# A channel shuffle that streams 64 MB through SBUF: other tile sizes at its two ends

## The chip, the core and the metric

One of the eight cores of a Trainium2 chip runs the whole kernel. The metric is the device time of one execution in microseconds (us). Five executions of the kernel before gave a median of 317.01 us, with 316.95 us as the lowest and 317.26 us as the highest.

## The reference

The input `x` is a float32 array of 16 x 64 x 64 positions with 256 channels each, 67.11 MB in all. The 256 channels are 8 groups of 32. The result holds the same values with the two channel axes exchanged, at every position by itself:

```python
x = x.reshape(batch, h, w, groups, channels_per_group)   # 8 x 32
x = x.transpose(0, 1, 2, 4, 3)                           # 32 x 8
x = x.reshape(batch, h, w, c)
```

No arithmetic is done. Every byte has to be read from HBM once, be moved within its row of 256 channels, and be written to HBM once.

## The kernel before

The 65,536 positions are seen as rows of 256 floats, 1 KB each. The kernel cuts them into tiles of 128 x q rows: each of the 128 SBUF partitions gets q whole rows that lie next to each other in HBM, so a tile has q KB in each partition and 128 q KB in all. The list `_SIZES` on line 12 gives q for each tile in order, and its sum has to be 512 (65,536 / 128). There are 24 tiles before the change: 4, 8 and 16 KB a partition, then twenty of 24 KB (3.15 MB each), then one of 4 KB.

For each tile the loop does three things, in program order:

- line 47: SyncE's queue (SP) issues one transfer from HBM into `in_tile`;
- line 49: VectorE (DVE) copies `in_tile` to `out_tile` and exchanges the two channel axes by the order in which the copy reads;
- line 53: ScalarE's queue (ACT) issues one transfer from `out_tile` to HBM.

No other instruction works on the data. There are four `in_tile` buffers and four `out_tile` buffers, each as large as the biggest tile whatever the tile's size. So the first four loads are issued at once, and load k+4 waits until copy k has read its buffer. Copy k waits for load k to land, and, from the fifth tile on, for store k-4 to have left its buffer. Store k waits for copy k. Each queue issues in order: SP has only loads, ACT has only stores. The order of the program is the order in which the loop writes it; no scheduler moves anything.

The text numbers tiles, loads, copies and stores from 0 to 23. Each transfer is 128 packets, one for each partition's q KB, which are spread over the core's 16 DMA engines, 8 packets to each engine, and one packet of 4 bytes on each engine that reports the end. So the size of a tile is also the size of its packets.

Of the kernel before, what the change touches and what calls it, by code (L numbers as in the profile page):

```python
# [1 line left out]

# [4 lines left out]


F32 = mybir.dt.float32
P = 128  # L10

_SIZES = [4, 8, 16] + [24] * 20 + [4]
_IN_BUFS = 4
_OUT_BUFS = 4


@with_exitstack
def kernel(
    ctx: ExitStack,
    tc: tile.TileContext,  # L20
    x: bass.AP,
    groups: bass.AP,
    out: bass.AP,
):
    nc = tc.nc
    b, h, w, c = x.shape
    G = int(groups)
    CPG = c // G
    assert G * CPG == c
    assert sum(_SIZES) * P == b * h * w  # L30
    biggest = max(_SIZES)

    x_flat = x.rearrange("b h w c -> (b h w c)")
    out_flat = out.rearrange("b h w c -> (b h w c)")

    in_pool = ctx.enter_context(tc.tile_pool(name="in_pool", bufs=_IN_BUFS))
    out_pool = ctx.enter_context(tc.tile_pool(name="out_pool", bufs=_OUT_BUFS))

    def rows(flat, first, q):

        return flat[first * c : (first + P * q) * c].rearrange("(p f) -> p f", p=P)

    ctx.enter_context(tc.manual_schedule(engines=None))
    first = 0
    for q in _SIZES:
        in_tile = in_pool.tile([P, biggest * c], F32, name="in_tile")
        nc.sync.dma_start(out=in_tile[:, : q * c], in_=rows(x_flat, first, q))  # L47
        out_tile = out_pool.tile([P, biggest * c], F32, name="out_tile")
        nc.vector.tensor_copy(  # L49
            out=out_tile[:, : q * c].rearrange("p (i j g) -> p i j g", j=CPG, g=G),  # L50
            in_=in_tile[:, : q * c].rearrange("p (i g j) -> p i j g", g=G, j=CPG),
        )
        nc.scalar.dma_start(out=rows(out_flat, first, q), in_=out_tile[:, : q * c])
        first += P * q


# [1 line left out]
_INS = ['x', 'groups']  # L58
_OUTS = [((16, 64, 64, 256), 'float32')]

_NUMBERS = {'groups': 8}


# [26 lines left out]
```

## Time and profile before

| what | value |
|---|---|
| median of five runs | 317.01 us (316.95 to 317.26) |
| time of the profiled execution | 317.26 us |
| its span in the profile | 315.5 us |
| what lies around the span | 1.76 us |
| VectorE busy | 121.8 us (39%), 24 copies |
| bytes read and written | 67.11 MB each |
| mean rate over the span | 425 GB/s |
| DMA queues | q1 (loads, issued by SP) and q10 (stores, issued by ACT), 3456 packets each |

The profile counts time from the start of the span. Busy time of an engine is the time in which its instructions run; a DMA's issue on SP or ACT takes some 0.3 to 0.4 us and is not counted as busy, while its data moves for much longer, so a transfer is read by its issue and by its landing (the moment at which all 16 engines have reported its end). The rate in GB/s adds both directions.

### The profile page before, as it was taken

What the parts mean: (1) busy time and instruction counts of PE and PEld (TensorE: products, weight loads), DVE (VectorE), ACT (ScalarE), POOL (GpSimd) and SP (SyncE); (2) the same over time, 40 slices, a digit from 0 to 9 for tenths busy, and PEclk for the clock granted to TensorE, in tenths of its full rate; (3) what the DMA queues carried; (4) which work ended last, traced back from release to release, by engine and by line L of the source; (5) the groups of instructions that cost most, each with busy time, mean ns of one, the idle gap of its engine ahead of it and who ended that gap; (6) DMA issues with size and microseconds to landing.
All of it is one profiled execution on the core that took longest, in us unless ns stands there. A gap on an engine that the chain in (4) does not pass through costs nothing.

```text
span 315.5 us, 178 instructions
## 1 busy us (share of the span) xinstructions
DVE 121.8 (39%) x24; POOL 0.2 (0%) x4
## 2 busy tenths in 40 slices
DVE  3435716244251707061533526070715244261710
POOL 0000000000000000000000000000000000000000
DMA  8999999999999999999999999999999999999997
GB/s 316 415 404 428 440 424 446 433 418 446 433 418 446 436 414 446 436 414 446 436 421 439 442 414 439 446 418 433 449 414 433 449 421 427 449 424 427 441 420 319
DMA packets 6912, 134.22 MB, mean 425 GB/s; under 512 B 768, under 2 KB 768, under 8 KB 1280
## 3 DMA queue, kind: packets, MB, share of 16 engines
q1 hardware_dynamic: 3456, 67.11, 49.8%
q10 hardware_dynamic: 3456, 67.11, 49.5%
HBM read 67.11 MB, written 67.11 MB: 425 GB/s over the span
## 4 chain that ended last, share of the span: by engine, by line
DMA 36%; another core or an unknown queue 33%; DVE 26%; SPq 0%; issue 0%; DVEq 0%
DMA in_tile<-in_x_dram 36%; DVE out_tile L49 26%; SPq L47 0%; DVEq L49 0%
## 5 line engine op out<-in xcount | busy, mean ns | idle before, releaser
L49 DVE COPY out_tile<-in_tile 128x6144 f32<-128x6144 f32 (+3 forms) x24 | 121.8, 5075 | 181.6 <-DMA in_tile<-in_x_dram 181.6
L71 POOL MEMSET const-bfloat16-1.0<- 128x1 bf16 x1 | 0.1, 102 | 0.0
L71 POOL MEMSET const-uint8-127<- 128x1 uint8 x1 | 0.1, 102 | 0.0
L71 POOL MEMSET const-float32-0.0<- 128x1 f32 x1 | 0.1, 100 | 0.2 <-issue 0.2
L71 POOL MEMSET const-float32-1.0<- 128x1 f32 x1 | 0.1, 99 | 0.0
## 6 DMA issues: line engine op xcount, KB each, us to landing
in_tile<-in_x_dram SPq DMA_DIRECT2D x20, 3072.0 KB, 52.3
out_dram<-out_tile ACTq DMA_DIRECT2D x20, 3072.0 KB, 31.8
in_tile<-in_x_dram SPq DMA_DIRECT2D x1, 2048.0 KB, 11.0
out_dram<-out_tile ACTq DMA_DIRECT2D x1, 2048.0 KB, 23.8
in_tile<-in_x_dram SPq DMA_DIRECT2D x2, 512.0 KB, 24.8
in_tile<-in_x_dram SPq DMA_DIRECT2D x1, 1024.0 KB, 5.3
out_dram<-out_tile ACTq DMA_DIRECT2D x2, 512.0 KB, 11.9
out_dram<-out_tile ACTq DMA_DIRECT2D x1, 1024.0 KB, 19.1
```

The source lines that it names most:

```text
L49: nc.vector.tensor_copy(out=out_tile[:, : q * c].rearrange("p (i j g) -> p i j g", j=CPG, g=G), in_=in_tile[:, : q * c].rearrange("p (i g ...
L71: nc = _bacc.Bacc("TRN2", target_bir_lowering=False, num_devices=1)
```

## The change

The list of tile sizes is replaced. There are again 24 tiles that sum to 512. At the start the three tiles of 4, 8 and 16 KB become four of 2, 4, 8 and 18 KB; the twenty tiles of 24 KB follow; the last tile of 4 KB is gone, so the last tile is now one of 24 KB. The buffers, the loop, the engines and the queues are untouched.

```diff
-_SIZES = [4, 8, 16] + [24] * 20 + [4]
+_SIZES = [2, 4, 8, 18] + [24] * 20
 _IN_BUFS = 4
 _OUT_BUFS = 4
```

On VectorE the first four copies become 128 x 512, 128 x 1024, 128 x 2048 and 128 x 4608 elements where they were 128 x 1024, 128 x 2048, 128 x 4096 and 128 x 6144, and the last one becomes 128 x 6144 where it was 128 x 1024. The loads on SP and the stores on ACT change in the same way.

## The prediction

> **What bounds the kernel now.** I read the page first: the span, the rate in 40 slices, the bytes and the costliest group.
>
> ```profile
> span 315.5 us, 178 instructions
> GB/s 316 415 404 428 440 424 446 433 418 446 433 418 446 436 414 446 436 414 446 436 421 439 442 414 439 446 418 433 449 414 433 449 421 427 449 424 427 441 420 319
> HBM read 67.11 MB, written 67.11 MB: 425 GB/s over the span
> L49 DVE COPY out_tile<-in_tile 128x6144 f32<-128x6144 f32 (+3 forms) x24 | 121.8, 5075 | 181.6 <-DMA in_tile<-in_x_dram 181.6
> ```
>
> The rate is flat from the second slice to the last but one, and VectorE, the only engine with work, sits idle for 181.6 us until loads land. At 433 GB/s, the rate of the middle, 134.22 MB take 310 us of the span of 315.5. So the DMA engines are the bound, and what is left is 5.5 us at the two ends and in the ramp. To see where, I cut the span by stages:
>
> ```profile
> 1.60:6.00 4.40, 1.09 (x1) 0.00 (x0) 1.00 0.97 380
> 6.00:10.50 4.50, 2.02 (x1) 0.00 (x0) 1.00 1.04 400
> 10.50:18.00 7.50, 3.89 (x1) 0.00 (x0) 1.00 1.00 428
> 18.00:20.00 2.00, 0.00 (x0) 0.00 (x0) 1.00 0.97 377
> 20.00:40.00 20.00, 11.35 (x2) 0.00 (x0) 1.00 1.01 427
> 40.00:280.00 240.00, 91.84 (x17) 0.00 (x0) 1.00 1.00 433
> 302.00:312.00 10.00, 1.09 (x1) 0.00 (x0) 1.00 1.00 433
> ```
>
> The last number is GB/s. From 40 us on nothing is lost, whether loads and stores mix (40 to 280) or stores are alone (302 to 312). Before that the ramp falls short of 433. In time that is 4.50 x (1 - 400/433) = 0.34 us, 7.50 x (1 - 428/433) = 0.09, 2.00 x (1 - 377/433) = 0.26 and 20 x (1 - 427/433) = 0.28: together 0.97 us between 6 and 40 us. From 1.60 to 6 us it is 0.54 us, the first packets' latency among it.
>
> Then the end, since that is where the last tile grows. The timeline from 280 us:
>
> ```profile
> 284.87 18.85 ACTq L53 DMA_DIRECT2D out_dram<-out_tile  x3
> 293.70 5.69 DVE L49 COPY out_tile<-in_tile 128x6144 f32<-128x6144 f32 x1 [8.86 <-DMA in_tile<-in_x_dram]
> 302.27 1.09 DVE L49 COPY out_tile<-in_tile 128x1024 f32<-128x1024 f32 x1 [2.88 <-DMA in_tile<-in_x_dram]
> ```
>
> and the stores issued at 284.9, 299.4 and 303.4 us (tiles 21, 22, 23), each with its time to landing:
>
> ```profile
> L53 ACTq DMA_DIRECT2D out_dram<-out_tile x1: 339/339/339, 284.9 to 284.9; - x1
> DMA to landing us min/median/max: 21.3/21.3/21.3
> ...
> L53 ACTq DMA_DIRECT2D out_dram<-out_tile x1: 338/338/338, 299.4 to 299.4; - x1
> DMA to landing us min/median/max: 14.0/14.0/14.0
> ...
> L53 ACTq DMA_DIRECT2D out_dram<-out_tile x1: 338/338/338, 303.4 to 303.4; - x1
> DMA to landing us min/median/max: 11.3/11.3/11.3
> ```
>
> They land at 306.2, 313.4 and 314.7 us. Store 23 carries 0.52 MB, 1.2 us at 433 GB/s, and takes 11.3: it stands in a queue. How long that queue is, the bytes of each queue in the first 293.70 us (the landing of load 22) tell:
>
> ```profile
> q1 hardware_dynamic: 3313, 66.59, 53.1%
> q10 hardware_dynamic: 2959, 59.09, 46.8%
> ```
>
> The stores are 66.59 - 59.09 = 7.50 MB behind the loads. I call this the backlog.
>
> **The change part by part.** My sum is made against the profiled execution, 317.26 us: span 315.5 plus 1.76 around it. It stands 0.25 us above the median of 317.01, so a difference found there is applied to 317.0.
>
> *Bytes and packets: 0.* There are 24 tiles and 512 KB a partition before and after, so 48 transfers, 134.22 MB and 6912 packets. Only the split changes. The packet records of the trace have medians of 159, 309, 611 and 912 ns for packets of 4, 8, 16 and 24 KB: a straight line, 8.5 ns plus 37.6 ns a KB. On it 2 KB cost 84 ns and 18 KB 686. Each engine has 8 packets of each tile and direction: before (4 + 8 + 16 + 4 KB) 159 + 309 + 611 + 159 = 1238 ns, after (2 + 4 + 8 + 18) 84 + 159 + 309 + 686 = 1238. If the 2 KB packets kept the 4 KB price, 16 of them would add 16 x 75 ns = 1.2 us; if the line holds or bends down, 0. I take the line, as it holds over the three steps shown, the nearest at 4 KB; 1.2 us is the upper bound.
>
> *VectorE: 0.* The copies take 1.09, 2.02, 3.89 and 5.69 us for 4, 8, 16 and 24 KB, a straight line again, so about 0.6 for 2 KB and 4.3 for 18 KB. The sum of the changed copies goes from 8.1 us to 8.0. Each lies beside DMA work, as the 181.6 us of idle time show, save the last one, which has its own term.
>
> *The start: 0, at most +0.4 us.* Loads 0 to 3 are issued at 0.73, 1.14, 1.62 and about 2.1 us, 0.4 to 0.5 apart, and the first packet moves at 1.75, so an issue takes 1.0 us to show. Load 0 of 2 KB is 8 packets x 84 ns = 0.7 us plus the 0.3 us of first latency that the packet records show, to about 2.7; load 1 can move at 2.2. No hole. A hole could not be longer than one issue step, 0.4 us. The first four loads now hold 32 KB a partition where they held 52. Alone they feed the engines to about 1.75 + 0.3 + 8 x 1.238 = 12 us. Load 4 waits for copy 0, which is done by 4 us (it ended at 5.07 before, with a load twice as long), so load 4 is queued 7 us early. SP and ACT have no other work that could be held.
>
> *The ramp: +0.1 us, between -1.0 and +1.0.* The 0.97 us shown above sit where loads are alone (6 to 10.5 us) or outweigh stores (18 to 40 us). After the change both stages differ. Store 0 is issued at about 4.0 us in place of 5.1, so loads are alone for about 1 us less: at 400 GB/s a gain of 1 x 33/433 = 0.1 us. But the stores that then pair with loads are of 2, 4, 8 and 18 KB, one tile more before the two sides are equal, which lengthens the loads' majority: in the stage of 20 to 40 us that costs 0.28/20 = 0.014 us a us, and one more tile pair of 14.5 us makes +0.2. The bounds are that the whole loss goes (-1.0) or comes a second time (+1.0). I take the sum of the two small terms, since they come from the nearest rows.
>
> *The end: 0.* Here a 4 KB tile, copied in 1.09 us, is replaced by one copied in 5.69. The copy is on the path only if the store queue runs dry before the store is issued. The trace of before shows this very case one tile earlier. Load 22, of 24 KB, lands at 293.70, its copy takes 5.69 us, and store 22 is issued at 299.4. It lands 14.0 us later, while 3.15 MB need 7.3 at 433 GB/s. So some 6 us of the 14.0 are time in the queue; the packet records have its first packet at 305.04, 5.6 us after the issue. Without load 23 beside it (0.52 MB, 1.2 us) that spare would be 4.4 us.
>
> After the change the spare is larger, because the backlog grows. An engine that has both queues full takes a packet of each in turn. The end shows it: between 293.70 and 302.2 us load 23 of 0.52 MB takes 8.5 us, as 3.17 MB of stores pass beside it, packet for packet. So while a store tile of small packets pairs with loads of large ones, the backlog grows by 128 x the difference in KB. Before: 2.87 MB are loaded in the first 9 us without a store; store 0 (4 KB) meets loads of 16 and 24 KB, about +2.0 MB; store 1 (8 KB) meets 24, +2.1; store 2 (16) meets 24, +1.05. Sum 8.0 MB, and 7.50 were read above just after a load ended, with 24 KB on both sides it swings by half a tile. After: 2.4 to 2.9 MB alone; 2 KB against 18, +2.1; 4 against 24, +2.6; 8 against 24, +2.1; 18 against 24, +0.8. Sum 10.0 to 10.5 MB, or 3.2 to 3.3 tiles. When load 23 lands, at least 10.0 - 3.15 = 6.9 MB of older stores are left, 15.8 us at 433 GB/s, less 1.35 us in which load 22's last packet (292.35) became a landing. Copy 23 and its issue take 5.75 us, so store 23 stands in the queue 8.7 us before its turn. Even an issue that takes 4.1 us to show, as store 0's does (issued 5.1, first packet 9.18), leaves 4 us. Four out buffers hold 3.3 tiles, so copies don't wait for them either. The term runs from 0 to the cost of a dry queue in the rivals.
>
> The Trainium skill has a rule that speaks against this step: DMA: Bandwidth & Descriptors, section "Anatomy of one DMA — SWDGE (gpsimd) path", fits one transfer as about 2.0 us plus its bytes at 436 GB/s. As an estimate from that page the last store would go from 3.2 us to 9.2 and the kernel to about 323 us. The rows (11.3 us for 0.52 MB, 14.0 for 3.15) disagree with it: they are queueing times, and the fit is of the other issue path.
>
> The sum: 0 + 0 + 0 + 0.1 + 0 on 317.0, so **317.1 us**.
>
> **The rivals.**
>
> *The last copy is exposed.* If the two queues were not served packet for packet, or the stores caught up during the run, store 23 would find an empty queue. With nothing ahead of it the price is 1.35 + 5.69 + the 1.0 us that an issue takes, about 8 us less the 1.2 of the old small tile: 323.8 us. It decides from the point where the older stores left at load 23's landing fall under (5.75 + 1.0) x 0.433 = 2.9 MB. Before there were, at 293.70, 67.11 - 59.09 - 3.15 - 0.52 = 4.35 MB. A near miss would cost 1 to 2 us, 318 to 319. Against it stand the 5.6 us of spare.
>
> *The ramp gets worse.* More stages of lopsided traffic, or 2 KB packets at the old price, bring the 0.97 us a second time: 318.0 us. The loss from 18 to 20 us, beside a store of 8 KB packets, speaks for it; the 428 GB/s of 10.5 to 18 us, where a 4 KB store meets loads, speaks against it.
>
> *The ramp gets better.* The stage at 400 GB/s is that of the 16 KB load, which is gone. If its size were the cause, 0.34 us return; if the whole ramp loss goes, the time is 316.0 us. Against it: 24 KB loads lose time too, from 18 us on.
>
> **How the numbers follow.** Measured against the spread of these runs (0.1%), 0.2% or 0.63 us is about what can be told from no change: 316.4 to 317.6. No change 0.62; the ramp worse 0.17; the last copy exposed 0.08; the ramp better 0.13. So faster 0.13, same 0.62, slower 0.25. The range takes both bounds of the ramp and leaves out the exposed copy and what lies beyond the bounds: 316.0 to 318.2.
>
> **What would show it.** In the changed profile the last copy should start at about 292 to 293 us and the last store be issued near 298 and land some 16 us later, at the end. Stores of 24 KB should take about 41 us to land in the middle (31.8 before), loads 52.4 as before, and the middle run at 433 GB/s with 14.55 us from copy to copy. Stores should be about 10 MB behind loads. A rate under 420 GB/s in a stage between the last copy's start and the end would mean the exposed copy; one between 6 and 40 us that differs from the rows above, one of the ramp rivals. The prediction falls if the store queue empties before the last store, if 2 KB or 18 KB packets leave the line, or if a backlog of 10 MB changes the rate in the middle, where each 1% would be 3 us.

## The result, and the profile after

The changed kernel takes 317.74 us (median of 26 runs, 316.88 to 318.44) against 316.99 us before (46 runs, 316.77 to 317.39). The medians differ by 0.75 us. The ratio of the runs is 1.0022, with a 95% interval of 1.0017 to 1.0028 (0.5 to 0.9 us), at the edge of the 0.2% (0.63 us) that the prediction called "no change"; the median lies just outside it. The second finding is the spread: single runs of the changed kernel lie within 1.56 us, those of the kernel before within 0.62.

The profiled execution is one of the faster ones, 317.40 us; the one before, 317.26, is one of the slower ones of its kernel. So the two pages show little of the 0.75 us:

```profile
span 315.6 us, 178 instructions
HBM read 67.11 MB, written 67.11 MB: 425 GB/s over the span
L49 DVE COPY out_tile<-in_tile 128x6144 f32<-128x6144 f32 (+4 forms) x24 | 121.6, 5066 | 177.2 <-DMA in_tile<-in_x_dram 177.2
```

The stages of the changed kernel, cut as before (the last number is GB/s):

```profile
1.60:6.00 4.40, 1.51 (x2) 0.00 (x0) 1.00 0.99 359
6.00:10.50 4.50, 2.23 (x2) 0.00 (x0) 1.00 1.01 410
10.50:18.00 7.50, 3.97 (x1) 0.00 (x0) 1.00 1.01 430
18.00:20.00 2.00, 0.35 (x1) 0.00 (x0) 1.00 1.06 442
20.00:40.00 20.00, 11.35 (x2) 0.00 (x0) 1.00 1.01 420
40.00:280.00 240.00, 92.23 (x17) 0.00 (x0) 1.00 1.00 432
302.00:312.00 10.00, 0.00 (x0) 0.00 (x0) 1.00 1.01 435
```

The middle and the stores alone at the end run at the old rate (432 and 435 GB/s, 433 and 433 before). What differs lies before 40 us: 359 for 380 GB/s in the first stage, 410 for 400 in the second, 442 for 377 from 18 to 20 us, and 420 for 427 from 20 to 40 us.

The end, first in the timeline and then in the last store:

```profile
278.54 5.76 DVE L49 COPY out_tile<-in_tile 128x6144 f32<-128x6144 f32 x1 [8.85 <-DMA in_tile<-in_x_dram]
284.33 14.83 ACTq L53 DMA_DIRECT2D out_dram<-out_tile  x2
293.13 5.65 DVE L49 COPY out_tile<-in_tile 128x6144 f32<-128x6144 f32 x1 [8.84 <-DMA in_tile<-in_x_dram]
```
```profile
L53 ACTq DMA_DIRECT2D out_dram<-out_tile x1: 339/339/339, 298.8 to 298.8; - x1
...
DMA to landing us min/median/max: 16.0/16.0/16.0
```

The last load lands at 293.13, the copy takes 5.65 us, and store 23 waits in a queue: it lands 16.0 us after its issue, of which its 3.15 MB need 7.3. The bytes of the two queues in the first 293.13 us show the backlog:

```profile
q1 hardware_dynamic: 3456, 67.11, 53.7%
q10 hardware_dynamic: 3052, 58.36, 46.3%
```

The stores are 8.75 MB behind, 5.6 MB of it older than store 23. That is 12.9 us of work, and the copy needs 5.65. The packet records have store 23's first packet at 306.3 us, 7.5 us after its issue. So the last copy is not exposed.

**Where the time of an execution is made.** The packet records give each packet's duration, and packets of one size have one undisturbed duration, their median (912 ns for 24 KB). Packets that take longer are late. Added up over an execution and divided by 16 engines, in us an engine:

| execution | loads late, before 45 us | loads late, after 45 us | stores late, before / after 45 us |
|---|---|---|---|
| before, 317.26 | 1.19 | 0.0 | 0.0 / 0.0 |
| changed, 317.40 | 1.48 | 0.0 | 0.0 / 0.0 |
| changed again, 316.86 | 1.29 | 0.0 | 0.0 / 0.0 |
| changed a third time, 317.41 | 1.38 | 0.0 | 0.0 / 0.0 |

Only loads are late, and only at the start. From 45 us on 24 KB packets start 908 or 909 ns apart, and some 914 ns from one tile to the next, so what an engine has lost by then it keeps to the end. The sum of late time is not by itself the time lost: "changed again" has 0.10 us more of it than before, and yet its engines end earlier (next table), since its first packets begin 0.09 us earlier on average and the spaces between packets differ too. A store has landed when the last of the 16 engines reports it, so the engine that lost most sets the end:

| execution | mean of the 16 engines' last landings | last of the 16 | device time | device time less last landing |
|---|---|---|---|---|
| before | 314.11 | 314.67 | 317.26 | 2.59 |
| changed | 314.24 | 314.81 | 317.40 | 2.59 |
| changed again | 314.04 | 314.27 | 316.86 | 2.59 |
| changed a third time | 314.33 | 314.82 | 317.41 | 2.59 |

The 0.14 us between the two profiled executions and the 0.54 between two of the changed kernel are, to 0.01, the difference of the last engine's landing. The changed kernel can be as fast as the old one (316.86) when its 16 engines end together, within 0.45 us here.

### The profile page after: what moved, and what is told of

Its sections match the earlier page's. It is cut to its first block, busy times and chain, and to the rows that moved or that the text cites. A ratio compares the mean times of both kernels' runs of the same rounds, so it can differ in the third digit from the quotient of the medians.

```text
span 315.6 us, 178 instructions
## 1 busy us (share of the span) xinstructions
DVE 121.6 (39%) x24; POOL 0.2 (0%) x4
## 4 chain that ended last, share of the span: by engine, by line
another core or an unknown queue 42%; DVE 31%; DMA 21%; issue 0%; DVEq 0%
DVE out_tile L49 31%; DMA in_tile<-in_x_dram 21%; DVEq L49 0%
## 5 line engine op out<-in xcount | busy, mean ns | idle before, releaser
L49 DVE COPY out_tile<-in_tile 128x6144 f32<-128x6144 f32 (+4 forms) x24 | 121.6, 5066 | 177.2 <-DMA in_tile<-in_x_dram 177.2
## 6 DMA issues: line engine op xcount, KB each, us to landing
out_dram<-out_tile ACTq DMA_DIRECT2D x20, 3072.0 KB, 38.5
```

The lines of the kernel that those rows point to most:

```text
L49: nc.vector.tensor_copy(out=out_tile[:, : q * c].rearrange("p (i j g) -> p i j g", j=CPG, g=G), in_=in_tile[:, : q * c].rearrange("p (i g ...
```

## The experiments

The theories were: the small tiles at the start cost it ("head"), the 24 KB tile at the end costs it ("end"), or the twenty 24 KB tiles cost it because they now begin four blocks of 128 rows later ("rows"). Each batch shared the runs of the kernel before, with medians of 316.93 to 317.00 us.

### The new head with the old end

```diff
-_SIZES = [4, 8, 16] + [24] * 20 + [4]
+_SIZES = [2, 4, 8, 14] + [24] * 20 + [4]
```

> Sizes 2, 4, 8, 14, twenty of 24, then 4 KB: the new small head with the old 4 KB end, and the 24 KB tiles at the old rows. Theory 'head' (loads outweigh stores for longer at the start, and this costs the 0.7 us and the wider spread of the runs): about 317.6 us, spread of the runs over 1 us. Theory 'end' (a 24 KB last tile costs it): 317.0 us with a spread of 0.6 us. Theory 'rows' (the 24 KB tiles start 4 row blocks later): 317.0 us.

Measured: 317.93 us (9 runs, 316.90 to 318.07), ratio 1.0023 (1.0014 to 1.0033). The head alone brings the whole difference and the spread. In its profile (317.68 us) the stage from 20 to 40 us is again the one that is short, and the middle is not:

```profile
20.00:40.00 20.00, 11.42 (x2) 0.00 (x0) 1.00 1.01 420
40.00:280.00 240.00, 94.93 (x17) 0.00 (x0) 1.00 1.01 433
```

The last landings have a mean of 314.32 us, 0.21 later than before, but the last one is at 315.05, 0.38 later, with the next to last at 314.48. One engine alone makes over half a microsecond of this execution's time.

### The small tile moved from the end to the start

```diff
-_SIZES = [4, 8, 16] + [24] * 20 + [4]
+_SIZES = [4, 8, 16, 4] + [24] * 20
```

> Sizes 4, 8, 16, 4, then twenty of 24 KB: the old head, with the small last tile moved to the fourth place, so that the last tile is of 24 KB and the 24 KB tiles start at the changed kernel's rows. Theory 'head': near 317.0 us, unless the 4 KB tile beside 24 KB loads makes a lopsided stage of its own (then up to 317.6). Theory 'end': 317.7 us. Theory 'rows': 317.7 us.

Measured: 317.26 us (11 runs, 317.10 to 317.38), ratio 1.0009 (1.0000 to 1.0018). Neither 317.0 nor 317.7: by itself it could have meant a small cost of the end. Its packet records put its loss elsewhere: its 16 KB loads are late by about 0.55 us an engine between 9.5 and 12.5 us (before 0.06), and no 24 KB packet is late by more than 0.02 us.

### The changed kernel again, and the rows

The changed kernel was run again, and the old sizes were run on the new rows:

```diff
-    for q in _SIZES:
+    for k, q in enumerate(_SIZES):
+        if k == 3:
+            first = 32 * P
+        if k == 23:
+            first = 28 * P
```

> The changed kernel once more, for a second profile and a second set of times on the same chip as the others of this batch. All theories: 317.7 us with single runs between 316.9 and 318.5. If the time of the profiled execution is over 317.9, its packet records should show where it differs from the first profile (317.40): in the ramp by 'head', after the last load by 'end', in the middle by 'rows'.

> The sizes and the order of the kernel before, but the last tile of 4 KB takes the rows after the 16 KB tile, so the twenty 24 KB tiles start 4 row blocks later, at the rows where the changed kernel has them. Theory 'rows': 317.7 us. Theories 'head' and 'end': 317.0 us with the old narrow spread.

Measured: the changed kernel 317.61 us (11 runs, 316.86 to 318.67), ratio 1.0017 (1.0006 to 1.0027); the old sizes on the new rows 317.00 (316.78 to 317.08), ratio 1.0000 (0.9992 to 1.0009). "Rows" falls. The profiled execution was the fastest of them, 316.86, so it shows nothing of the longer ones.

### The end alone

```diff
-_SIZES = [4, 8, 16] + [24] * 20 + [4]
+_SIZES = [4, 8, 16] + [24] * 20
...
-    assert sum(_SIZES) * P == b * h * w
+    assert sum(_SIZES) * P <= b * h * w
```

> Sizes 4, 8, 16, then twenty of 24 KB, and nothing more: the last 4 KB a partition of the kernel before are left out (neither read nor written), so the old head meets a 24 KB end. The 16 packets of 4 KB that each engine no longer moves are 16 x 155 ns = 2.5 us. If a 24 KB end is free: 317.0 - 2.5 = 314.5 us, with the narrow spread of the kernel before. If the end costs the 0.3 us by which the kernel with the small tile in fourth place was slower: 314.8 us. If the end costs all of the 0.7 us: 315.2 us.

Measured: 314.62 us (5 runs, 314.52 to 314.63) against 316.96. Less 2.5 us for the work left out, 0.1 to 0.2 us remain for a 24 KB end. Most of that lies behind the last landing: device time less last landing is 2.73 us here and 2.72 in the two other kernels with 23 tiles (4, 8, 20 and 8, 12, 16, 20, below), where the kernels with 24 tiles have 2.58 to 2.60, three of them with a 24 KB end. Why 23 tiles cost 0.13 us there was not asked. Its own end, in the timeline and the last store, looks like the old kernel's tile 22:

```profile
293.80 5.70 DVE L49 COPY out_tile<-in_tile 128x6144 f32<-128x6144 f32 x1 [8.87 <-DMA in_tile<-in_x_dram]
299.53 0.34 ACTq L53 DMA_DIRECT2D out_dram<-out_tile  x1
```
```profile
DMA to landing us min/median/max: 12.4/12.4/12.4
```

Even with the smaller backlog of the old head the last store stands in a queue: 12.4 us to its landing for 7.3 us of data.

### Three small tiles, and a gentle head

```diff
-_SIZES = [4, 8, 16] + [24] * 20 + [4]
+_SIZES = [4, 8, 20] + [24] * 20
```
```diff
-_SIZES = [4, 8, 16] + [24] * 20 + [4]
+_SIZES = [8, 12, 16, 20] + [24] * 19
```

> Sizes 4, 8, 20, then twenty of 24 KB: 23 tiles, a 24 KB end, and a head in which 24 KB loads meet a store of 8 KB packets for one tile only, as before. Theory 'lopsided' (time is lost while 24 KB loads meet stores of 8 KB and less): 317.0 us less 0.1 for one tile's packets fewer, narrow spread. Theory 'end': 317.3 or more.

> Sizes 8, 12, 16, 20, then nineteen of 24 KB: 23 tiles and no stage in which 24 KB loads meet stores under 12 KB. Theory 'lopsided': 316.6 to 316.9 us, with almost no loss between 18 and 40 us. Its rival, that the loss is made where loads are alone and of 12 KB or more (load 0 is larger, so the first store comes about 2 us later): 317.2 us or more.

Measured: 4, 8, 20 gives 317.02 us (11 runs, 316.86 to 317.13), ratio 1.0002 (0.9993 to 1.0011), with a 24 KB tile at its end. With the run before this settles the end: it costs 0.2 us at most. The gentle head gives 317.28 (316.91 to 317.46), ratio 1.0009 (1.0000 to 1.0018). "Lopsided" expected 316.9 at most. Not one of its 24 KB packets is late, as that theory said, but its 16 and 20 KB loads are, by 0.65 us an engine from 9.5 to 14.5 us and 0.23 from 19.5 to 23.5. Its rival's time (317.2 or more) came, but not quite its place: only half of the late 16 KB load time, 0.33 us, falls before the first store's packets at 11.5 us, where loads are alone.

### Lopsided traffic far from the start

```diff
-_SIZES = [4, 8, 16] + [24] * 20 + [4]
+_SIZES = [4, 8, 16] + [24] * 7 + [2] + [24] * 6 + [2] + [24] * 7
```

> The kernel before with its last tile of 4 KB cut into two tiles of 2 KB and put far apart in the middle (after 7 and after 13 of the 24 KB tiles), so that two stages of some 8 us have 24 KB loads beside 2 KB stores, far from the start; two more packets a tile and engine add 0.1 us. Theory 'lopsided': each stage loses 0.1 to 0.4 us, so 317.3 to 317.9 us with a wide spread. Theory 'ramp alone' (the loss needs the state of the engines after the start, not the mix): 317.1 us, and no loss in the packet records of the two stages.

Measured: 317.07 us (11 runs, 316.99 to 317.32), ratio 1.0004 (0.9995 to 1.0012). The two small stores go out from 134 to 142 and from 223 to 231 us, beside 24 KB loads. The stages around them:

```profile
130.00:142.00 12.00, 6.50 (x2) 0.00 (x0) 1.00 1.02 438
142.00:219.00 77.00, 28.70 (x7) 0.00 (x0) 1.00 1.00 432
219.00:231.00 12.00, 6.48 (x2) 0.00 (x0) 1.00 0.98 421
231.00:290.00 59.00, 24.38 (x5) 0.00 (x0) 1.00 1.00 432
```

In such short windows the rate depends on which packets begin inside (the kernel before has 432 and 428 in the same two), so the packet records decide: between 45 and 300 us no packet is late by as much as 20 ns. Loads of 24 KB beside stores of 2 KB are not late by themselves. "Lopsided" by itself falls; the loss belongs to the start.

### What in the head: the 2 KB, or the fourth small tile

```diff
-_SIZES = [4, 8, 16] + [24] * 20 + [4]
+_SIZES = [4, 4, 8, 16] + [24] * 20
```
```diff
-_SIZES = [4, 8, 16] + [24] * 20 + [4]
+_SIZES = [2, 8, 18] + [24] * 20 + [4]
```

> Sizes 4, 4, 8, 16, then twenty of 24 KB: four small tiles as in the changed kernel, but the first is of 4 KB. The first 24 KB load is then the fifth, issued after copy 0, as in the changed kernel. Theory 'fourth small tile' (the loads run on through 24 KB packets while a fourth small store goes out, and the load packets that are late then cost the slowest engine): 317.5 to 317.8 us with a spread over 0.8 us. Theory 'first tile of 2 KB': 317.0 us, narrow.

> Sizes 2, 8, 18, twenty of 24, then 4 KB: three small tiles and the old end, but the first tile is of 2 KB. The first 24 KB load is the fourth, issued at once, as before. Theory 'first tile of 2 KB' (the first store comes a microsecond earlier and its small packets leave the engines out of step): 317.5 to 317.8 us, wide. Theory 'fourth small tile': 317.0 us, narrow.

Measured: 4, 4, 8, 16 gives 317.48 us (11 runs, 317.23 to 318.28), ratio 1.0019 (1.0010 to 1.0027), slower and wide without a 2 KB tile. Its profiled execution is one of the longer ones, 318.01 us, and shows the slowest engine at work: mean of the last landings 314.38, the last at 315.42, four others between 314.7 and 314.9. The other, 2, 8, 18, gives 317.14 (12 runs, 316.82 to 317.50 and one of 319.21), ratio 1.0010 (0.9999 to 1.0021): unclear, but nearer to the old kernel.

The third profile of the changed kernel, of a single execution:

> The changed kernel, one more profile, in the hope of an execution near its median of 317.7 us. What every theory left expects: no loss after 45 us, and the time above the fastest execution explained by the slowest of the 16 DMA engines: its last landing lies 2.6 us before the device time, as in the profiles so far (314.83 for 317.40, 314.29 for 316.86).

Its execution took 317.41 us, with the last landing at 314.82. The difference of 2.59 held (the expectation's two landings stand 0.02 us late against the profile's zero: they are 314.81 and 314.27); an execution of the changed kernel at or above its median was never profiled.

### A fifth small tile

```diff
-_SIZES = [4, 8, 16] + [24] * 20 + [4]
+_SIZES = [2, 2, 4, 8, 16] + [24] * 20
```

> Sizes 2, 2, 4, 8, 16, then twenty of 24 KB: five small tiles ahead of the 24 KB ones, where the changed kernel has four and the kernel before three; one tile more than the changed kernel adds 0.1 us of packets. Theory 'number of small tiles ahead' (each small tile adds a stage at the start in which the 16 engines lose unequal time, and the slowest sets the end): 318.0 us or more, spread over 1 us. Rival, that the step from three to four alone does it, since four loads are issued at once and the first 24 KB load is then no longer among them: 317.5 to 317.8 us, like the changed kernel. If five small tiles give 317.1, neither stands.

Measured: 318.35 us (5 runs, 317.74 to 318.64), ratio 1.0037 (1.0023 to 1.0050). Its first three stages and the long ones:

```profile
1.60:6.00 4.40, 1.23 (x2) 0.00 (x0) 1.00 0.93 244
6.00:10.50 4.50, 1.19 (x2) 0.00 (x0) 1.00 1.01 411
10.50:18.00 7.50, 3.91 (x2) 0.00 (x0) 1.00 1.03 436
...
20.00:40.00 20.00, 11.49 (x2) 0.00 (x0) 1.00 1.01 432
40.00:280.00 240.00, 96.29 (x17) 0.00 (x0) 1.00 1.01 433
```

and those of 4, 4, 8, 16:

```profile
1.60:6.00 4.40, 1.86 (x2) 0.00 (x0) 1.00 0.96 330
6.00:10.50 4.50, 1.81 (x2) 0.00 (x0) 1.00 1.03 380
10.50:18.00 7.50, 3.28 (x2) 0.00 (x0) 1.00 0.99 418
```

Here the loss is in the first 10 us (244 GB/s against 380 before), where the third and fourth of the small loads (4 and 8 KB) have late packets, up to 1.5 us late; 20 to 40 us is clean at 432. The mean of the last landings is 314.82, 0.71 later than before, and the last is at 315.71, 1.05 later. That is nearly the difference of the two profiled executions (318.35 and 317.26, 1.09). Late packets are only 0.36 us an engine of the 0.71; the packets of one more tile add 0.16, and the rest lies in the spaces between packets.

Set side by side, by the number of tiles under 24 KB ahead of the long run:

| small tiles ahead | heads, median us |
|---|---|
| 3 | 4, 8, 16: 316.99 (on other rows 317.00); 4, 8, 20: 317.02; 2, 8, 18: 317.14 |
| 4 | 4, 8, 16, 4: 317.26; 8, 12, 16, 20: 317.28; 4, 4, 8, 16: 317.48; 2, 4, 8, 18: 317.74; 2, 4, 8, 14: 317.93 |
| 5 | 2, 2, 4, 8, 16: 318.35 |

By their medians all heads of four are above all of three, and five is above all of four. The number is not all: within the four, those that begin with 2 KB are the slowest. And the two fastest heads of four, at 0.3 us more, have intervals that begin at 1.0000 and overlap with that of 2, 8, 18; only the other three, and the head of five, are clearly slower than the kernel before.

## Why the prediction was right or wrong

The time of 317.74 us lies in the range of 316.0 to 318.2. It is not in the likeliest case (316.4 to 317.6, chance 0.62) but between it and the rival "the ramp gets worse" (318.0, chance 0.17). That rival was near in time, but neither of its two reasons held: 2 KB packets kept to the line, and lopsided traffic in the middle lost nothing.

*Bytes and packets, 0:* right. The packet records of the changed kernel have medians of 84 ns for 2 KB and 686 for 18 KB, the values read off the line.

*VectorE, 0:* right. Copies of 0.63 and 4.32 us (0.6 and 4.3 foreseen), and the idle time is still all for loads.

*The end, 0:* right, and shown by the end alone (0.1 to 0.2 us) and by 4, 8, 20 with a 24 KB end (317.02). The last copy began at 293.13 (292 to 293 foreseen), its store was issued at 298.8 (298) and landed 16.0 us later (16). The backlog came out a little under the sum: in the packet records it is 9.4 to 10.1 MB in the middle (10.0 to 10.5 foreseen), 2.2 MB of it loaded ahead of the first store (2.4 to 2.9 foreseen), and 24 KB stores took 38.5 us to land where about 41 were foreseen. At the landing of load 23 it is down to 8.75 MB, since hardly anything but stores moves in the last 1.35 us before. The prediction's aside that the backlog swings by half a tile was too large: before, it ran from 7.5 to 8.3 MB, a quarter of a tile. The fit of a DMA's time in the Trainium skill (DMA: Bandwidth & Descriptors, "Anatomy of one DMA — SWDGE (gpsimd) path"), which by the prediction's estimate would have made it about 323 us, does not apply here: a last transfer six times as large added 0.2 us at most.

*The start, 0 to +0.4, and the ramp, +0.1 between -1.0 and +1.0:* this is the step that failed, in size. The ramp and the start together cost the 0.75 us, less the 0.2 at most of the end, where 0.1 was the sum. That lies within the bounds, which is owed to their width: the value taken was the sum of two small terms from the mean rate of the stages. The first, a gain of 0.1 for a shorter time with loads alone, and the second, +0.2 for one more lopsided tile pair, have the right sign and are too small: in late load time the changed kernel's three profiles (executions of 316.9 to 317.4 us, under its median) have 0.13 to 0.22 us an engine from 6 to 10.5 us (before 0.48) and 0.55 to 0.74 from 20 to 40 us (0.23). A third, in the first stage up to 6 us, was put at nothing and is 0.35 to 0.56 (0.27). The reason given, lopsided traffic, is not enough: it loses nothing far from the start. The loss goes with late load packets of the first 45 us, at places that differ from head to head (9.5 to 12.5 us for 4, 8, 16, 4; before 10 us for 2, 2, 4, 8, 16), and the end is set by the engine that lost most, not by the mean. A mean rate can't show that: in the execution of the new head with the old end, 0.21 us of the 0.38 us are seen in the mean, the rest in one engine.

*The spread:* not foreseen. The prediction took the profiled execution, 0.25 us above its median, as good for the whole. For the changed kernel one profile is worth less: its three lay 0.3 to 0.9 us below its median of 317.74.

*What stays open:* why load packets are late at the start and never later. The place was found, a fourth small tile was clearly slower in three heads of five, and the mix of sizes far from the start was shown to cost nothing. Whether it is the reading of HBM, the preparing of so many transfers in so short a time, or the order in which the engines fall out of step was not told apart. Nor was the number of small tiles separated from the fact that the first 24 KB load is then no longer among the four issued at once; the fifth small tile speaks for the number, as it cost more again, but it starts with two tiles of 2 KB. All five heads of four have that late first 24 KB load and range from 317.26 to 317.93, so it does not set the size of the loss alone. That the slowest engine makes the changed kernel's own longer executions, and so the 0.75 us of its median, is argued from neighbours (317.68, 318.01 and 318.35 us), since its own profiles were all of faster executions.

## What to carry to other kernels

In a stream that the DMA engines bound from end to end, the last copy and store cost nothing while older stores still queue ahead of them, so read the queue at the last load's landing before shrinking the last tile. At the start, do not add small tiles beyond what fills the pipe: here no head of three was clearly slower than the kernel before, three of five heads of four were, and the one of five was the slowest. Fewer than three were not tried. And where 16 engines share a transfer, look at the last of them and at several executions: the mean rate of one profile hides both.

## What was not expected of the hardware

After the first 45 us the DMA engines were exact to a few nanoseconds: 24 KB packets 908 or 909 ns apart within a tile for 250 us, loads and stores mixed, or stores alone, with no packet over 0.04 us late in 13 of the 14 profiled executions (in that of 4, 4, 8, 16 single stores were up to 0.11 us late, 0.03 us an engine in all). Nearly all late time lay in loads of the first 45 us, and what it made of the last landing reached the device time unchanged: device time less last landing was 2.58 to 2.60 us in all kernels with 24 tiles, 2.63 to 2.64 in those with 25 and 2.72 to 2.73 in those with 23. And with two tiles of 2 KB ahead of 4 and 8 KB, single load packets were up to 1.5 us late, and the first 4.4 us of transfers ran at 244 GB/s.
